# A hybrid attention layer on one core: load buffers in one ring, two weight loads moved back, scalings of queries and keys one step later

## The chip, the cores and the metric

The kernel runs on one core of a Trainium2 chip. The core has a matrix engine (PE in the profile; its weight loads are the row PEld), a vector engine (DVE), an activation engine (ACT), a general engine (POOL) and a queue engine (SP), which here issues nearly all DMA transfers from HBM into the on-chip SBUF. Each engine works through its own instruction list in order. They wait for one another through semaphores. The metric is the device time of one execution in microseconds, and lower is better.

## What is computed

A decoder layer for 256 tokens of width 2048, in float32: an adaLN modulation, one input projection to 9296 columns, two groups of eight heads each with a gate, and one output projection.

```python
mod = jax.nn.silu(c) @ w_ada + b_ada
shift, scale, gate = jnp.split(mod, 3, axis=-1)
h = _rms_norm(x, g_norm) * (1.0 + scale[:, None, :]) + shift[:, None, :]
proj = h @ w_in
qa, ka, va, za, q_idx, k_idx, w_idx, qb, kb, vb, zb = jnp.split(proj, COL_SPLITS, axis=-1)
...
ya = _dsa_attention(qa, ka, va, q_idx, k_idx, w_idx, _alibi_slopes(N_HEADS_A))
yb = _moba_attention(qb, kb, vb, _alibi_slopes(N_HEADS_B))
ya = ya.reshape(B, L, D_A) * jax.nn.silu(za)
yb = yb.reshape(B, L, D_B) * jax.nn.silu(zb)
y = jnp.concatenate([ya, yb], axis=-1) @ w_out
return x + gate[:, None, :] * y
```

With 256 tokens the second group sees one causal block. The first group keeps, for each query, the 64 keys that an indexer of 16 small heads scores highest. Scores get a penalty of slope times distance, and the slope of head n is 2 to the power of -(n+1).

## The kernel before

**Products.** Each float32 weight is split into two parts: a cast on ACT gives `wh` (L322) and a subtraction on DVE gives `wl` (L332). The activations are split alike (`hhi`, `hlo`). Three matmuls make one product: L774 (`wh` by `hhi`), L775 (`wl` by `hhi`) and L776 (`wh` by `hlo`). So no matmul of a weight piece beyond its L774 can run before both ACT and DVE have worked on that piece. Weights arrive in `raw` buffers of 1 MB, issued by SP (`issue`, L243). `wh` and `wl` have four buffers each.

**Modulation.** `w_ada` comes through the same `raw` buffers; DVE takes the dot product of each 128 x 2048 block with one instruction (`gemv`, L289). `between` (L182) decides after how many weight blocks (`n_kt`) these loads stand in the list of loads.

**Start.** The first row block of the input (k = 0) is used by itself, for the four groups of b1 (`zb1`, `qb1`, `kb1`, `vb1`: one quad of 128 x 512 weights in one load, pieces 0 to 3) and those of a0 (`za0`, `qa0`, `ka0`, `va0`: pieces 4 to 7). Then come pieces of two row blocks: 8 to 11 for a1, 12 for `i2` and so on. A finished sum leaves PSUM by an ACT copy (`evac`, L675) into `p_za0_0`, `p_za0_1` and so on, one for each half of the tokens. Sums have four PSUM buffers.

**Background tasks.** Beside the matmuls of a piece, one step of each background task is put out (`Bg.step`, L588). `prep` (L500) is one such task: eight squares on ACT (L506), a mean and a power on POOL (L149, L150), then eight scalings on ACT (L513); its first `yield` says how many pieces lie between. `idx_pair` (L461) copies two indexer heads out of PSUM (`qi`, L468) and makes their logits (`lg`, L474, L475). `head` (L524) runs from a transposition (`tr`) over scores (`s`, L540), a softmax on DVE and ACT (L545, L548) and a transposition (`pt`, L554) to the product with the values (`pv`, L563). For its penalty POOL makes a table `nb` (L536).

**Order.** The code's order is a wish: a scheduler with its own model of durations places each engine's instructions, and what it decided is fixed when the kernel is built. `in_order` pins some of it. The `raw` buffers are a pool of four (`rawp`) and a pool of two (`rawe`), which is given back when the first late tile is made; before that `rawe` serves the modulation loads in `EARLY`.

## Time and profile before

| | |
|---|---|
| median of three runs | 575.06 us (574.56 to 578.45) |
| profiled execution | 578.7 us, of which the traced span is 576.9 us |
| mean granted PE clock | 0.995 |
| PE busy | 553.6 us, 96% of the span |
| DVE, ACT, POOL busy | 444.5, 319.6 and 48.0 us |
| DMA | 150.09 MB, mean 260 GB/s |

The busy time of PE counts overlapping matmuls once. The profile also has a chain of waits followed back from the last instruction, a table of what each engine waited for, and the instructions in order of time. In rows of the timeline the first number is the start in us from the beginning of the span, the second the time to the end of the last of the xcount instructions in the row; what stands in brackets is the engine's idle time before the row, and who ended it.

### The profile page before, as it was taken

How to read it: one execution, taken by the hardware profiler on the slowest of the kernel's cores; microseconds unless marked ns; L12 is line 12 of the kernel's file. 1: busy time of each engine (PE TensorE's matmuls, PEld its weight loads, DVE VectorE, ACT ScalarE, POOL GpSimd, SP SyncE). 2: the span in 40 equal slices, each digit the busy share in tenths (PEclk: the TensorE clock that was granted, in tenths of full speed). 3: DMA queues.
4: the chain of work that ended last, by engine and by line, in shares of the span. 5: the costliest groups of instructions: out<-in, count | busy, mean ns of one | idle time of the engine just before them, and what ended most of it. 6: DMA issues, size and time to landing. Idle time of an engine off the chain costs nothing.

```text
span 576.9 us, 7456 instructions
## 1 busy us (share of the span) xinstructions
PE 553.6 (96%) x2658; PEld 462.7 (80%) x2658; DVE 444.5 (77%) x683; ACT 319.6 (55%) x652; POOL 48.0 (8%) x62
## 2 busy tenths in 40 slices
PE   3889999999999999999799999999999999999996
PEld 2769888888889988976577888888888888887885
DVE  4877789898898898998689996678787576458452
ACT  4588563544444353576555566646776785554340
POOL 4100000000000000102201002111110210000000
PEclk9999999999999999999989999999999999999999
DMA  8999998898898987877845376767675468445611
GB/s 293 412 350 370 361 346 326 330 360 285 314 359 318 366 326 270 268 298 279 303 152 177 129 275 235 273 221 265 226 255 201 148 231 279 146 150 190 244 37 38
DMA packets 59670, 150.09 MB, mean 260 GB/s; under 512 B 3056, under 2 KB 9456, under 8 KB 53616
## 3 DMA queue, kind: packets, MB, share of 16 engines
q1 hardware_dynamic: 58480, 147.51, 71.1%
q10 hardware_dynamic: 1152, 2.10, 1.2%
q8 instruction: 21, 0.34, 0.2%
q14 instruction: 17, 0.14, 0.1%
HBM read 147.50 MB, written 2.10 MB: 259 GB/s over the span
## 4 chain that ended last, share of the span: by engine, by line
PE 87%; ACT 4%; DVE 2%; POOL 2%; issue 2%; DMA 1%; SPq 0%; DVEq 0%; ACTq 0%
PE mm_y_o L774 5%; PE mm_y_o L776 5%; PE mm_y_o L775 5%; PE mm_h_zb L776 3%; PE mm_h_zb L774 3%; PE mm_h_zb L775 3%; PE mm_h_za L775 3%; PE mm_h_i L776 3%; PE mm_h_i L775 3%; PE mm_h_i L774 3%; PE mm_h_qb L774 3%; PE mm_h_za L776 3%; PE mm_h_qb L776 3%; PE mm_h_qb L775 3%; PE mm_h_qa L774 3%; PE mm_h_ka L775 2%
## 5 line engine op out<-in xcount | busy, mean ns | idle before, releaser
L322 ACT ACTIVATE wh<-raw 128x1024 fp32r<-128x1024 f32 (+3 forms) x192 | 188.2, 990 | 140.5 <-PE mm_y_o L776 32.9
L332 DVE TENSOR_TENSOR wl<-raw,wh 128x1024 fp32r<-128x1024 f32 (+3 forms) x192 | 215.0, 1140 | 60.5 <-ACT wh L322 59.9
L289 DVE CUSTOM_DVE_ANT_0 raw<-raw,s_row 128x2048 f32<-128x2048 f32 (+1 forms) x49 | 110.2, 2250 | 14.1 <-DMA raw<-in_w_ada_t 14.1
L774 PE MATMUL mm_y_o<-wh,yT 128*128 128x512 f32 x128 | 51.7, 404 | 0.0
L775 PE MATMUL mm_y_o<-wl,yT 128*128 128x512 f32 x128 | 49.9, 390 | 0.0
L776 PE MATMUL mm_y_o<-wh,yT 128*128 128x512 f32 x128 | 49.8, 390 | 0.0
L774 PE MATMUL mm_h_i<-wh,hhi 128*128 128x384 f32 (+1 forms) x96 | 31.7, 330 | 0.0
L775 PE MATMUL mm_h_i<-wl,hhi 128*128 128x384 f32 (+1 forms) x96 | 31.5, 328 | 0.0
L536 POOL TENSOR_SCALAR nbb<-dist 128x384 f32<-128x384 f32 x8 | 8.0, 1001 | 283.3 <-DVE mmod L289 211.2
L776 PE MATMUL mm_h_i<-wh,hlo 128*128 128x384 f32 (+1 forms) x96 | 31.4, 329 | 0.0
L776 PEld LDWEIGHTS mm_y_o<-wh,yT 128*128 128x128 f32 x128 | 24.0, 188 | 5.4 <-DVE yT L575 0.2
L774 PEld LDWEIGHTS mm_y_o<-wh,yT 128*128 128x128 f32 x128 | 24.1, 188 | 4.7 <-ACT yT L574 0.2
L775 PEld LDWEIGHTS mm_y_o<-wl,yT 128*128 128x128 f32 x128 | 24.1, 188 | 4.6
L774 PE MATMUL mm_h_qa<-wh,hhi 128*128 128x512 f32 x64 | 25.6, 409 | 0.9 <-ACT wh L322 0.9
L774 PE MATMUL mm_h_zb<-wh,hhi 128*128 128x512 f32 x64 | 26.4, 412 | 0.0
L774 PE MATMUL mm_h_vb<-wh,hhi 128*128 128x512 f32 x64 | 26.4, 412 | 0.0
L775 PE MATMUL mm_h_za<-wl,hhi 128*128 128x512 f32 x64 | 25.1, 392 | 0.9 <-DVE wl L332 0.9
L774 PE MATMUL mm_h_kb<-wh,hhi 128*128 128x512 f32 x64 | 25.7, 405 | 0.0
L775 PE MATMUL mm_h_zb<-wl,hhi 128*128 128x512 f32 x64 | 25.7, 401 | 0.0
L775 PE MATMUL mm_h_vb<-wl,hhi 128*128 128x512 f32 x64 | 25.6, 400 | 0.0
L774 PE MATMUL mm_h_qb<-wh,hhi 128*128 128x512 f32 x64 | 25.5, 401 | 0.0
L774 PE MATMUL mm_h_za<-wh,hhi 128*128 128x512 f32 x64 | 25.5, 406 | 0.0
(216 smaller groups left out, 1227.3 us busy)
## 6 DMA issues: line engine op xcount, KB each, us to landing
raw<-in_w_in SPq DMA_DIRECT2D x51, 1024.0 KB, 5.9
raw<-in_w_ada_t SPq DMA_DIRECT2D x47, 1024.0 KB, 6.2
raw<-in_w_out SPq DMA_DIRECT2D x16, 1024.0 KB, 5.0
raw<-in_w_in SPq DMA_DIRECT2D x17, 512.0 KB, 3.6
raw<-in_w_in SPq DMA_DIRECT2D x11, 768.0 KB, 4.6
x<-in_x SPq DMA_DIRECT2D x8, 256.0 KB, 6.9
xr<-in_x ACTq DMA_DIRECT2D x8, 256.0 KB, 6.5
raw<-in_w_in SPq DMA_DIRECT2D x3, 672.0 KB, 7.4
```

What stands on the lines that cost most here:

```text
L289: nc.vector.tensor_tensor_reduce(out=ld["v"], in0=ld["v"], in1=s_row[:, h0:h1], scale=1.0, scalar=0.0, op0=ALU.mult, op1=ALU.add, accum_ou ...
L322: nc.scalar.activation(hi[:, :n, :w], v, AF.Copy)
L332: nc.vector.tensor_tensor(lo[:, :n, :w], v, sb["hi"][:, :n, :w].bitcast(F32), op=ALU.subtract)
L536: nc.gpsimd.tensor_scalar(nb, dista if q[0] == "a" else dist, 2.0 ** -(hid + 1), 0.0, op0=ALU.mult, op1=ALU.add)
L774: nc.tensor.matmul(ps, a_hi, sb["hi"][:, i, :w], start=st, stop=False)
L775: nc.tensor.matmul(ps, a_hi, sb["lo"][:, i, :w], start=False, stop=False)
L776: nc.tensor.matmul(ps, a_lo, sb["hi"][:, i, :w], start=False, stop=en)
```

## The change

Six things are changed. (1) The first four modulation loads after the start are no longer all ahead of the a0 quad: two stand ahead of it, two behind. (2) The six `raw` buffers are used in turn; after the pool of two is given back, five are used in turn, four old ones and one in the late pool. (3) `prep` waits one piece longer before its scalings. (4) The `nb` tables are gone: the softmax instruction scales the distance itself, and the key's factor comes from a table of eight columns, made on POOL, of which one belongs to each head. (5) Four temporaries take other buffers: `junkx` the `u` tiles, and `qi`, `th` and the output's `o` the two `qk` buffers. (6) Since every one of these moves something in the scheduler's model, instructions change place that the diff does not touch. All L-numbers of matmuls and copies grow by ten.

```diff
-ADA_AT, ADA_FIRST, ADA_GAP, ADA_LAG, GATE_AT, GATE_GAP = 4, 4, 5.5, 2, 150, 8
-EARLY = {1, 2} | set(range(5, 2 * KT + KT * KT))
+ADA_FIRST, ADA_AT, ADA_GAP, ADA_LAG, GATE_AT, GATE_GAP = (4, 4, 8, 8), 9.5, 5.5, 2, 150, 8
...
     gneg = {}
+    steep = consts.tile([P, 8], F32, name="steep")
+    for h in range(8):
+        nc.gpsimd.memset(steep[:, h:h + 1], -(HD ** -0.5) * 2.0 ** (h + 1))
     for i, g in enumerate("ab"):
-        gt = consts.tile([P, 1], F32, name=f"gneg{g}")
-        nc.vector.scalar_tensor_tensor(gt, cc[:, 64 + 2 * i:65 + 2 * i], -(HD ** -0.5),
-                                       cc[:, 65 + 2 * i:66 + 2 * i], op0=ALU.mult, op1=ALU.mult)
+        gt = consts.tile([P, 8], F32, name=f"gneg{g}")
+        nc.gpsimd.tensor_scalar(gt, steep, cc[:, 64 + 2 * i:65 + 2 * i], cc[:, 65 + 2 * i:66 + 2 * i],
+                                op0=ALU.mult, op1=ALU.mult)
...
-            pool = rawe if ld["kind"] == "ada" and ld["to"][0] == "mod" and n_issued - n_start in EARLY else rawp
-            raw = pool.tile([P, 2048], F32, tag="raw", name=f"raw{n_issued}")
+            pool = rawe if not late_pool and n_issued % 6 > 3 else rawp
+            if late_pool and n_issued % 5 == 4:
+                raw = late_pool[0].tile([P, 2048], F32, tag="raw", bufs=1, name=f"raw{n_issued}")
+            else:
+                raw = pool.tile([P, 2048], F32, tag="raw", name=f"raw{n_issued}")
...
-            junk = work.tile([P, 512], F32, name=f"junkx{t}{j}", tag="big", bufs=2)
+            junk = u_tile(f"junkx{t}{j}")
...
-        qi = late_tiles().tile([P, L], F32, name=f"qi{p}", tag="qi")
+        qi = late_tiles().tile([P, 512], F32, name=f"qi{p}", tag="qk", bufs=2)[:, :L]
...
         rsqrt(ssq[:, 8:16], ssq[:, 0:8], HD)
-        yield 1
+        yield 2
...
-        nc.scalar.activation(qk[:, L:], pt[:, L:], AF.Copy, scale=gneg[q[0]])
-        nb = late_tiles().tile([P, 384], F32, name="nb" + name, tag="nb", bufs=2)
-        nc.gpsimd.tensor_scalar(nb, dista if q[0] == "a" else dist, 2.0 ** -(hid + 1), 0.0,
-                                op0=ALU.mult, op1=ALU.add)
+
+        nc.scalar.activation(qk[:, L:], pt[:, L:], AF.Copy, scale=gneg[q[0]][:, hid:hid + 1])
+        far = dista if q[0] == "a" else dist
...
-            nc.vector.tensor_tensor_reduce(out=ns[:, lo:hi], in0=ps[:, lo:hi], in1=nb[:, lo:hi], scale=1.0,
+            nc.vector.tensor_tensor_reduce(out=ns[:, lo:hi], in0=ps[:, lo:hi], in1=far[:, lo:hi],
+                                           scale=2.0 ** -(hid + 1),
```

Where the instructions stand on three engines, at three places, follows.

**The start.** On ACT, from the copies of `qa0` on, before:

```order
L675 ACTIVATE p_qa0_1_404<-mm_h0_qa0_1_395 128x512
L322 ACTIVATE wh8_413<-raw9_300 128x1024
L675 ACTIVATE p_ka0_0_425<-mm_h0_ka0_0_417 128x512
L675 ACTIVATE p_ka0_1_427<-mm_h0_ka0_1_418 128x512
L675 ACTIVATE p_va0_0_446<-mm_h0_va0_0_438 128x512
L322 ACTIVATE wh9_434<-raw11_304 128x1024
L675 ACTIVATE p_va0_1_448<-mm_h0_va0_1_439 128x512
L322 ACTIVATE wh10_452<-raw12_306 128x1024
L675 ACTIVATE p_za1_0_470<-mm_h0_za1_0_456 128x512
L322 ACTIVATE wh11_476<-raw13_308 128x1024
L675 ACTIVATE p_za1_1_472<-mm_h0_za1_1_457 128x512
```

The same stretch of ACT now:

```order
L685 ACTIVATE p_qa0_1_406<-mm_h0_qa0_1_397 128x512
L685 ACTIVATE p_ka0_0_434<-mm_h0_ka0_0_426 128x512
L685 ACTIVATE p_ka0_1_436<-mm_h0_ka0_1_427 128x512
L685 ACTIVATE p_va0_0_455<-mm_h0_va0_0_447 128x512
L685 ACTIVATE p_va0_1_457<-mm_h0_va0_1_448 128x512
L332 ACTIVATE wh8_422<-raw9_309 128x1024
L685 ACTIVATE p_za1_0_479<-mm_h0_za1_0_465 128x512
L685 ACTIVATE p_za1_1_481<-mm_h0_za1_1_466 128x512
L332 ACTIVATE wh9_443<-raw11_313 128x1024
L332 ACTIVATE wh10_461<-raw12_413 128x1024
L332 ACTIVATE wh11_485<-raw13_415 128x1024
```

The casts 8, 9 and 10 moved behind copies of sums: `wh8` behind both copies of `va0`, `wh9` behind both of `za1`.

On DVE, from the second modulation block's sums to the subtraction of piece 4, before:

```order
L403 TENSOR_TENSOR mmod1_310<-mmod1_310,cc_79 128x1
L289 ISA raw6_219,mmod2_313<-raw6_219,s_row_113 128x2048
L289 ISA mmod2_313 128x1
L418 TENSOR_TENSOR hlo1_337<-xnT1_248,hhi1_334 128x256
L289 ISA raw7_221,mmod2_313<-raw7_221,s_row_113 128x2048
L289 ISA mmod2_313 128x1
L332 TENSOR_TENSOR wl4_318<-raw8_223,wh4_316 128x512
```

The same stretch of DVE now:

```order
L413 TENSOR_TENSOR mmod1_315<-mmod1_315,cc_79 128x1
L342 TENSOR_TENSOR wl4_320<-raw6_228,wh4_318 128x512
L428 TENSOR_TENSOR hlo1_339<-xnT1_257,hhi1_336 128x256
L342 TENSOR_TENSOR wl5_352<-raw6_228,wh5_350 128x512
L342 TENSOR_TENSOR wl6_373<-raw6_228,wh6_371 128x512
L299 ISA raw7_230,mmod2_419<-raw7_230,s_row_113 128x2048
L299 ISA mmod2_419 128x1
L342 TENSOR_TENSOR wl7_394<-raw6_228,wh7_392 128x512
```

The two dot products stood ahead of `wl4`; now one stands behind `wl6` and the other behind `wl7`.

**The keys of b0.** On ACT, from the last square of `kb0` to the next casts, before:

```order
L506 ACTIVATE jkb013_2532,sskb0_2517<-p_kb0_1_775 128x128
L513 ACTIVATE p_kb0_0_773<-p_kb0_0_773,sskb0_2517 128x128 x3
L468 ACTIVATE qi3_2559<-ptq3_2556 128x256
L513 ACTIVATE p_kb0_0_773<-p_kb0_0_773,sskb0_2517 128x128
L513 ACTIVATE p_kb0_1_775<-p_kb0_1_775,sskb0_2517 128x128 x4
L322 ACTIVATE wh106_2605<-raw98_2398 128x1024
```

The same stretch of ACT now:

```order
L516 ACTIVATE jkb013_2541,sskb0_2526<-p_kb0_1_784 128x128
L523 ACTIVATE p_kb0_0_782<-p_kb0_0_782,sskb0_2526 128x128 x2
L332 ACTIVATE wh106_2606<-raw98_2399 128x1024
L478 ACTIVATE qi3_2568<-ptq3_2565 128x256
L523 ACTIVATE p_kb0_0_782<-p_kb0_0_782,sskb0_2526 128x128 x2
L523 ACTIVATE p_kb0_1_784<-p_kb0_1_784,sskb0_2526 128x128 x4
```

The first scaling still follows the last square, and the cast `wh106` came ahead of `qi3`.

**The last head.** On PE, from the last two matmuls ahead of the scores of `a13` to the product with its values, now (before, the twelve matmuls of `wh172` and `wl172` stood between `sa13` and `pva12`, and seven of piece 174 between `pta13` and `pva13`):

```order
L786 MATMUL mm_y8_o0_1_4381<-wh172_4650,yT5_4674 128x512
L549 MATMUL sa13_4728<-qka13_4682 128x128
L550 MATMUL sa13_4728<-qka13_4682 128x256
L573 MATMUL pva12_4741<-pTa12_4705,p_va1_0_566 128x256
L575 MATMUL pva12_4741<-pTa12_4705,p_va1_1_568 128x128
L578 MATMUL pva12_4741<-ident_81,p_za1_0_479 128x128
L578 MATMUL pva12_4741<-ident_81,p_za1_1_481 128x128
L784 MATMUL mm_y8_o1_0_4538<-wh174_4712,yT4_4585 128x512
L564 MATMUL pta13_4752<-ident_81,nsa13_4731 128x128
L785 MATMUL mm_y8_o1_0_4538<-wl174_4714,yT4_4585 128x512
L564 MATMUL pta13_4752<-ident_81,nsa13_4731 128x128 x2
```

The twelve matmuls of piece 172 now run ahead of the scores, and between scores and transposition lie `pva12` and one matmul.

## Rows read from the trace of the kernel before

**Rows 1.** The profile's chain of waits: share of the span by engine
```profile
PE 87%; ACT 4%; DVE 2%; POOL 2%; issue 2%; DMA 1%; SPq 0%; DVEq 0%; ACTq 0%
```
**Rows 2.** What PE waited for: us in total, times, longest us
```profile
PE lg L474 <- ACT qi L468: 4.4, 2, 3.2
PE mm_h_za L775 <- DVE wl L332: 0.9, 1, 0.9
PE mm_h_qa L774 <- ACT wh L322: 0.9, 1, 0.9
...
PE sb L540 <- ACT rl L477: 0.3, 1, 0.3
PE ptk L457 <- ACT kk L452: 0.2, 1, 0.2
```
**Rows 3.** Busy time by stretches: PE, PEld, DVE, ACT, POOL, granted clock, DMA share, GB/s
```profile
40.00:240.00 200.00, 199.83 (x946) 172.02 (x947) 172.84 (x201) 100.58 (x139) 1.29 (x3) 1.00 0.90 329
...
280.00:300.00 20.00, 16.61 (x78) 12.37 (x77) 12.49 (x21) 10.32 (x26) 4.18 (x2) 0.91 0.55 180
...
320.00:560.00 240.00, 239.94 (x1155) 199.95 (x1155) 170.14 (x297) 145.41 (x344) 26.93 (x24) 1.00 0.61 211
```
**Rows 4.** Timeline of ACT at the start
```profile
28.14 1.28 ACT L675 ACTIVATE p_vb<-mm_h_vb 128x512 f32<-128x512 f32 x2 [0.99 <-PE mm_h_vb L776]
...
30.82 2.19 ACT L322 ACTIVATE wh<-raw 128x512 fp32r<-128x512 f32 x4
...
38.45 0.61 ACT L675 ACTIVATE p_va<-mm_h_va 128x512 f32<-128x512 f32 x1
38.93 1.08 ACT L322 ACTIVATE wh<-raw 128x1024 fp32r<-128x1024 f32 x1
```
**Rows 5.** Timeline of DVE at the start
```profile
30.73 2.28 DVE L289 CUSTOM_DVE_ANT_0 raw<-raw,s_row 128x2048 f32<-128x2048 f32 x1
...
32.94 2.49 DVE L332 TENSOR_TENSOR wl<-raw,wh 128x512 fp32r<-128x512 f32 x4
...
38.11 1.22 DVE L332 TENSOR_TENSOR wl<-raw,wh 128x1024 fp32r<-128x1024 f32 x1
```
**Rows 6.** Timeline of PE at the start
```profile
30.95 1.16 PE L373 MATMUL ptx<-diag,x 128*128 128x128 f32 x8 [0.38 <-ACT xnT L379]
...
38.35 0.39 PE L776 MATMUL mm_h_va<-wh,hlo 128*128 128x512 f32 x1
38.58 0.63 PE L774 MATMUL mm_h_za<-wh,hhi 128*128 128x512 f32 x2
...
43.16 0.39 PE L775 MATMUL mm_h_qa<-wl,hhi 128*128 128x512 f32 x1
```
**Rows 7.** Timeline of ACT, POOL and DVE at the scalings of `kb0`
```profile
285.24 0.98 ACT L513 ACTIVATE p_kb<-p_kb,sskb 128x128 f32<-128x128 f32 x3 [4.39 <-POOL sskb L150]
...
281.26 3.94 POOL L150 TENSOR_TENSOR sskb<-sskb,mhalf 128x8 f32<-128x8 f32 x1
...
281.43 2.28 DVE L289 CUSTOM_DVE_ANT_0 raw<-raw,s_row 128x2048 f32<-128x2048 f32 x1
```
**Rows 8.** L150 on POOL by tiles: least/median/most ns, first and last start
```profile
L150 POOL TENSOR_TENSOR ssqa<-ssqa,mhalf x2: 1635/1635/1635, 409.8 to 456.4; 128x8 f32<-128x8 f32 x2
```
**Rows 9.** Busy time by stretches after the long wait, columns as in rows 3
```profile
288.00:290.00 2.00, 2.00 (x6) 1.55 (x5) 1.07 (x1) 2.00 (x3) 0.00 (x0) 0.51 0.03 11
290.00:292.00 2.00, 2.00 (x9) 1.54 (x7) 2.00 (x5) 0.59 (x2) 0.00 (x0) 0.63 0.00 0
```
**Rows 10.** Timeline of PE and ACT at the last head
```profile
515.25 0.58 PE L774 MATMUL mm_y_o<-wh,yT 128*128 128x512 f32 x1
...
519.06 0.49 PE L554 MATMUL pta<-ident,nsa 128*128 128x128 f32 x3
...
516.49 0.49 ACT L548 ACTIVATE nsa<-nsa,sta 128x256 f32<-128x256 f32 x1
...
519.66 0.48 ACT L556 ACTIVATE pTa<-pta 128x384 f32<-128x384 f32 x1
```

## The prediction on record

> **What bounds the kernel now.** I read the chain of waits first. It is PE for 87% of the span [rows 1], so time is won or lost only where PE stands still or runs slowly. The second view is PE's busy time by stretches: from 40 to 240 us PE is busy 199.83 of 200 us, from 320 to 560 us 239.94 of 240 [rows 3]. These 440 us hold nothing to win, whatever ACT, DVE, POOL or the DMA queues do there. From 280 to 300 us PE is busy only 16.61 us and its granted clock averages 0.91. The third view says what PE waited for [rows 2]: 4.4 us for copies of indexer heads (`qi`) in two places, 3.2 and 1.2 us long; twice 0.9 us at the start for a subtraction and a cast; 0.3 and 0.2 us at two small places. The reader is to see how little this is: 6.7 us in all, about 1.2% of the time, and every edit has to be priced against these few waits or against new ones.

> The long wait is told by its rows [rows 7]. ACT has put the eight scalings of `kb0` right behind their squares, sits idle for 4.39 us until POOL's power ends, does three scalings, and only then copies `qi`. [...]

> **The change, part by part.** *The start.* The a0 quad stands two modulation loads earlier and DVE subtracts `wl4` before the two dot products instead of after them. Before, the first cast starts only at about 30.82 us, and `wl4` at 32.94, behind a dot product of 2.28 us [rows 4, 5]. Now one small copy lies between the copies of `vb1`, which end at 28.14 + 1.28 = 29.4, and the cast of piece 4: the cast (2.19 / 4 = 0.55) ends near 30.4, `wl4` (2.49 / 4 = 0.62) near 31.05. From there 22 matmuls at 0.23 (38.35 to 38.58 [rows 6]) and one transposition of the input, 0.9 by the stretch that starts at 30.95, take PE to the end of `va0` at about 37.0. Before, its last matmul starts at 38.35. So PE gains 1.5 us here.

> Then it loses more. `wh8` now stands behind both copies of `va0`. The second sum is done at 37.3, its copy (0.61 [rows 4], less a little overlap) at 37.9, and the cast of 1024 columns (1.08) at 38.95. PE has nothing to do from 37.0 to 38.95: 1.9 us. The two matmuls with `wh8` end at 39.4, but `wl8` (1.22 [rows 5]) only at 40.15: 0.75 us. Ten matmuls lead to 42.45. `wh9` stands behind both copies of `za1`, so: sum 42.65, copy 43.2, cast 44.25, another 1.8 us of idle PE. Two matmuls, 0.5 us of waiting for `wh10`, one matmul, and `wl9` is used first at 45.45. Before, it is used first at 43.16 [rows 6], with one matmul (0.23) less done by then. The start thus costs 45.45 - 0.23 - 43.16 = **+2.1 us**. Bounds: 0, if copies overlap so well that the lead of 1.5 lasts, and +3.8, if one of the gaps also brings 1.7 us of half clock. The gaps of 1.9 lie nearer to the 1.2 that brought no fall than to the 3.2 that did, so I take 2.1.

> [...]

> *Scalings later.* For `qb0` the extra step works: casts 99 and 100 now run while ACT would wait for POOL, and `qi1` has one cast of 1.05 less ahead of it. I take -0.95 of the 1.2 us wait (bounds 0 and -1.2). For `kb0` it does not: the scheduler still has the first scaling right behind the last square, so the 4.39 us stay. Moreover `wh106` (1.08) now stands ahead of `qi3`, in place of one scaling (0.98 / 3 = 0.33): **+0.7 us** (0 to +1.1), and the half clock stays. Heads also run one piece later; transpositions and scores thus leave the place where the 0.3 us wait was: -0.3 (0 to -0.3). Casts 94 and 95 go ahead of the key's copy `kk`, which frees the 0.2.

> *The last head.* Its scores now come behind piece 172. From the end of the scores (515.25) to the end of the second exponential (516.49 + 0.49) lie 1.7 us [rows 10]. The old cover was 3.8 us (to 519.06): 12 matmuls, 2.75, and `pva12`, 1.05. Now it is `pva12`, two matmuls and one transposition, about 1.6. The copy `pTa` ends at 520.14, some 0.85 after the transpositions; now three matmuls (0.7) stand there. Together with a semaphore or two **+0.5 us** (0 to +1.3, if a cast of 1.06 comes in between on ACT). Behind it nothing waits, so it reaches the end.

> *At nothing.* The ring: transfers are not among PE's waits [rows 2], and the later loads of the start are wanted 4 us or more after the buffer before them comes free. If one were late, PE would wait for up to a whole block: 1.05 MB at the 329 GB/s of the long stretch, 3.2 us. `nb` and the key's factors: they free POOL and cost it some memsets, while the heads' stretch has PE busy 239.94 of 240; bounds 0 and -0.1. The moved temporaries lie under the same cover.

> [...]

> Sum: +2.1 - 0.95 + 0.7 - 0.3 - 0.2 + 0.5 = +1.85 us. On the profiled execution this is 578.7 + 1.85 = 580.55; that one lies 3.6 above the median of the three runs, so for the median I say 575.06 + 1.85 = 576.9.

> **The rivals.** *The start keeps its lead.* If ACT's copies of `va0` and `za1` overlap with the matmuls and casts 8 and 9 end a microsecond earlier each, the start costs nothing: 574.8. For it: the two old waits of 0.9 are gone. Against it: the order in which the copies stand.

> *The long wait goes.* If the scalings of `kb0` no longer hold up `qi3`, the 3.2 us and the 1.7 of half clock vanish and the +0.7 with them: 576.9 - 5.6 = 571.3. Only with a free start as well would it be 569.2. A smaller form: the power beside no dot product takes 1.64 instead of 3.94; the wait is 2.3 shorter and the clock may hold: 572.9 to 574.6. Against both: the order of ACT and that of DVE, where the dot product still follows the sums of heads 4 and 5.

> *The start falls to half clock (slower).* Between 37.0 and 45.45 us PE would be idle for 5 of 8.4 us, in four pieces. If gaps of this size bring the fall that the one of 3.2 us brought, half clock comes once or twice, +1.7 each: 578.6 to 580.3, and with the upper bound of the last head 581.1. It decides from the second fall on. [...]

> *The change does nothing measurable.* The terms have both signs and each is under half a per cent; with the runs of one kernel spread from 574.56 to 578.45, 575 is as good an answer as 577.

> **How the numbers follow.** A measurement of this kernel can tell about 1%, 5.75 us, from no change. Forecast (575.5 to 579): 0.5. Start keeps its lead, or nothing: 0.2, within 1%. Long wait gone or shorter: 0.14, of which half goes beyond 1% with a free start or a lucky median: 0.07 faster, 0.07 within. Half clock at the start: 0.16, of which 0.12 beyond 580.8, since a slow run can be the median. So faster 0.08, same 0.8, slower 0.12. The range from 571.3 (long wait gone) to 581.1 (second fall and the last head) leaves out less than 2 in 10. The forecast's own is 575.5 to 579.

> **What would show it.** Right: in the profile after, PE waits near 37, 42.5 and 45 us for casts on ACT, 1.5 us or more each for two of them; the wait for `qi` at 269 us is under 0.5; the one at 287 us is 3.5 to 4.3 with ACT again waiting for POOL, and half clock behind it; the last head has waits of a few tenths near 520 us. Wrong: no idle PE between 37 and 46 us, a granted clock under 1 there, no long wait at 287 us, or PE waiting for a DMA anywhere, which the ring would then have caused.

## The result, and the profile after

| | before | after |
|---|---|---|
| median of six runs | 575.6 us (574.56 to 578.45) | 584.12 us (580.0 to 585.99) |
| profiled execution | 578.7 us | 585.07 us |
| span, granted PE clock | 576.9 us, 0.995 | 583.3 us, 0.98 |
| busy PE, DVE, ACT, POOL | 553.6, 444.5, 319.6, 48.0 us | 557.9, 443.1, 319.6, 32.2 us |

The ratio of the times is 1.0132, with an interval of 1.0102 to 1.0162 (the quotient of the two medians is 1.0148). The kernel became slower by 1.3%. The prediction said 576.9 us and at most 581.1, so it was wrong.

The medians lie 8.5 us apart, the profiled executions 6.4: that of before is one of its longer ones. The six times of after spread from 580.0 to 585.99, and one of these executions is traced. What follows explains the 6.4 us between two traced executions.

The chain of waits by engine, to be set beside [rows 1]:

```profile
PE 89%; ACT 4%; POOL 2%; DVE 1%; DMA 1%; issue 1%; SPq 0%; DVEq 0%; ACTq 0%
```

What PE waited for in the kernel after (us in total, times, longest us); this answers [rows 2]:

```profile
PE lg L484 <- ACT qi L478: 5.5, 2, 2.8
...
PE mm_h_za L784 <- ACT wh L332: 1.7, 1, 1.7
PE mm_h_qa L784 <- ACT wh L332: 1.6, 1, 1.6
PE mm_h_i L785 <- DVE wl L342: 0.7, 1, 0.7
PE mm_h_za L785 <- DVE wl L342: 0.5, 1, 0.5
PE mm_h_ka L784 <- ACT wh L332: 0.2, 1, 0.2
```

These are 10.2 us, where before had 6.7 (the waits ahead of the first products, for the modulation and the first transpositions, are left out of both). Of the 6.4 us between the two profiled executions they explain 3.5 at first sight. The clock adds to them. Busy time of the kernel after by stretches (columns as in [rows 3]: us, then PE, PEld, DVE, ACT, POOL, granted clock, DMA share, GB/s):

```profile
40.00:240.00 200.00, 197.31 (x919) 168.32 (x918) 169.42 (x197) 99.00 (x132) 0.00 (x0) 0.99 0.91 332
320.00:560.00 240.00, 240.00 (x1162) 200.30 (x1161) 173.15 (x323) 145.97 (x350) 11.88 (x12) 1.00 0.60 206
...
260.00:280.00 20.00, 17.25 (x73) 12.90 (x72) 16.77 (x25) 11.70 (x36) 6.09 (x2) 0.83 0.61 213
280.00:300.00 20.00, 17.23 (x80) 12.75 (x79) 12.01 (x18) 12.01 (x36) 4.19 (x2) 0.91 0.72 263
```

The heads' stretch holds nothing, as before. What is new are two stretches with a clock below 1. The same view in steps of 2 us shows both, first at the start, then behind the wait for `qi`:

```profile
44.00:46.00 2.00, 1.79 (x5) 1.31 (x5) 2.00 (x3) 1.26 (x2) 0.00 (x0) 0.65 0.22 36
46.00:48.00 2.00, 2.00 (x6) 1.52 (x6) 2.00 (x2) 0.60 (x1) 0.00 (x0) 0.50 0.92 310
48.00:50.00 2.00, 2.00 (x10) 1.61 (x9) 1.11 (x2) 0.60 (x1) 0.00 (x0) 1.00 0.94 352
274.00:276.00 2.00, 1.93 (x9) 1.28 (x10) 2.00 (x2) 1.21 (x3) 0.00 (x0) 0.50 0.00 0
276.00:278.00 2.00, 2.00 (x6) 1.52 (x6) 2.00 (x5) 0.62 (x2) 0.00 (x0) 0.50 0.87 250
278.00:280.00 2.00, 2.00 (x6) 1.61 (x5) 2.00 (x4) 0.00 (x0) 0.00 (x0) 0.50 1.05 409
```

At half clock (granted clock 0.50) PE is 100% "busy" and does about half the work: 6 matmuls in 2 us where 10 or 11 stand at a clock of 1.00. So the busy column hides it. The first fall costs 0.35 x 2 + 0.5 x 2 = 1.7 us, the second 3 x 0.5 x 2 = 3 us. With the 3.5 us of waits this is more than 6.4; an earlier beginning and smaller places take the excess off again.

**Where the time went.** The same matmul is looked up in both traces and its two starts are subtracted. This gives a ledger of PE's delay (start before, start after, difference, in us; pieces of one group are counted through):

```
41st transposition of the input      28.62   27.54   -1.09
first matmul of i                    50.87   53.86   +3.00
17th matmul of qb                    88.97   92.98   +4.00
33rd matmul of qb                   228.89  232.89   +4.00
logits before qb0's wait            261.10  264.47   +3.37
logits behind qb0's wait            269.07  274.07   +4.99
transposition after the half clock  272.80  280.57   +7.78
logits behind kb0's wait            286.54  293.82   +7.28
last part of the program            534.27  540.63   +6.36
```

So: start +4.0 (its beginning, 1.1 earlier, is already taken off), then -0.6 up to `qb0`, +1.6 in its wait and +2.8 in the half clock behind it, -0.5 in the wait of `kb0`, -0.9 behind that, and nothing at the last head. The sum is +6.4, which is 585.07 less 578.7. The loss has two places, the start and `qb0`. The earlier beginning need not come from the change: a second execution of before, shown below, is 0.9 us early at the same transposition, and against that one the start costs +4.9.

**The start.** PE's timeline in the kernel after, where it waits, beside [rows 6]:

```profile
37.98 0.73 PE L784 MATMUL mm_h_za<-wh,hhi 128*128 128x512 f32 x2 [1.67 <-ACT wh L332]
39.23 0.50 PE L785 MATMUL mm_h_za<-wl,hhi 128*128 128x512 f32 x1 [0.53 <-DVE wl L342]
...
43.42 0.73 PE L784 MATMUL mm_h_qa<-wh,hhi 128*128 128x512 f32 x2 [1.63 <-ACT wh L332]
44.37 0.62 PE L784 MATMUL mm_h_ka<-wh,hhi 128*128 128x512 f32 x1 [0.21 <-ACT wh L332]
...
61.15 0.45 PE L785 MATMUL mm_h_i<-wl,hhi 128*128 128x384 f32 x1 [0.74 <-DVE wl L342]
```

The four gaps at 38 to 44 us stand where they were forecast and have nearly the forecast lengths (1.9, 0.75, 1.8, 0.5). The half clock follows them directly. The wait at 61.15 was not foreseen: the subtraction that it needs stands behind a dot product of 2.29 us on DVE, which starts at 57.93 behind `hlo` of the second modulation chunk.

**The scalings.** The first group shows POOL's power (L152) at `qb0`, ACT's scalings that wait for it, DVE's instructions beside it, and PE's wait that follows. Below it stand the power and the dot product at `kb0`, which answer [rows 7]:

```profile
262.85 5.77 POOL L152 TENSOR_TENSOR ssqb<-ssqb,mhalf 128x8 f32<-128x8 f32 x1
...
268.65 1.28 ACT L523 ACTIVATE p_qb<-p_qb,ssqb 128x128 f32<-128x128 f32 x4 [4.13 <-POOL ssqb L152]
...
261.69 1.40 DVE L489 SCALAR_TENSOR_TENSOR sc<-rl,w,sc 128x128 f32<-128x128 f32 x4
263.01 0.69 DVE L531 SCALAR_TENSOR_TENSOR p_zb<-thb,p_zb 128x512 f32<-128x512 f32 x1
263.62 3.49 DVE L342 TENSOR_TENSOR wl<-raw,wh 128x1024 fp32r<-128x1024 f32 x3
...
274.07 0.81 PE L484 MATMUL lg<-kiT,qi 64*128 64x128 f32 x4 [2.75 <-ACT qi L478]
...
287.88 3.95 POOL L152 TENSOR_TENSOR sskb<-sskb,mhalf 128x8 f32<-128x8 f32 x1
...
288.05 2.28 DVE L299 CUSTOM_DVE_ANT_0 raw<-raw,s_row 128x2048 f32<-128x2048 f32 x1
```

The power on 128x8 numbers takes 1.64 us alone [rows 8]. Here it takes 5.77, and it ends at 268.62, 1.5 us after the third subtraction `wl` ends at 267.11. During all that time DVE goes from one instruction with two SBUF inputs to the next without a pause; the short `sc`, beside the last of which the power starts, has two as well (`rl` and `sc`). In the kernel before, the power at `qb0` took only 2.51 us. ACT starts the scalings late, the next `qi` comes behind them, PE is idle for 2.75 us, and the half clock follows.

### The profile page after: what moved, and what is told of

It is laid out like the page before. It is cut to its first block, busy times and chain, and to the rows that moved or that the text cites. A ratio compares the mean times of both kernels' runs of the same rounds, so it can differ in the third digit from the quotient of the medians.

```text
span 583.3 us, 7421 instructions
## 1 busy us (share of the span) xinstructions
PE 557.9 (96%) x2658; PEld 465.5 (80%) x2658; DVE 443.1 (76%) x681; ACT 319.6 (55%) x652; POOL 32.2 (6%) x56
## 4 chain that ended last, share of the span: by engine, by line
PE 89%; ACT 4%; POOL 2%; DVE 1%; DMA 1%; issue 1%; SPq 0%; DVEq 0%; ACTq 0%
PE mm_y_o L784 5%; PE mm_y_o L785 5%; PE mm_y_o L786 5%; PE mm_h_zb L784 3%; PE mm_h_za L785 3%; PE mm_h_zb L785 3%; PE mm_h_ka L785 3%; PE mm_h_zb L786 3%; PE mm_h_qa L785 3%; PE mm_h_qa L786 3%; PE mm_h_za L786 3%; PE mm_h_qb L784 3%; PE mm_h_qb L786 3%; PE mm_h_ka L786 3%; PE mm_h_ka L784 2%; PE mm_h_va L784 2%
## 5 line engine op out<-in xcount | busy, mean ns | idle before, releaser
L784 PE MATMUL mm_h_ka<-wh,hhi 128*128 128x512 f32 x64 | 25.8, 408 | 0.2 <-ACT wh L332 0.2
L785 PE MATMUL mm_h_qa<-wl,hhi 128*128 128x512 f32 x64 | 25.7, 402 | 0.0
L786 PE MATMUL mm_h_kb<-wh,hlo 128*128 128x512 f32 x64 | 25.7, 402 | 0.0
L786 PE MATMUL mm_h_qa<-wh,hlo 128*128 128x512 f32 x64 | 25.7, 402 | 0.0
L785 PE MATMUL mm_h_kb<-wl,hhi 128*128 128x512 f32 x64 | 25.7, 401 | 0.0
```

Source lines behind the costliest of these rows:

```text
L784: nc.tensor.matmul(ps, a_hi, sb["hi"][:, i, :w], start=st, stop=False)
L785: nc.tensor.matmul(ps, a_hi, sb["lo"][:, i, :w], start=False, stop=False)
L786: nc.tensor.matmul(ps, a_lo, sb["hi"][:, i, :w], start=False, stop=en)
```

## The experiments

For the start one reason stood first: the split of the modulation loads alone, through its gaps and the half clock. For `qb0` two were set against each other. One said that the later scalings let two casts through, whose subtractions then run beside the power. The other said that the scalings have no part in it, and that another of the edits moved instructions on DVE.

**Only the split, in the kernel before.** Only the places of the modulation loads are those of the kernel after:

```diff
-ADA_AT, ADA_FIRST, ADA_GAP, ADA_LAG, GATE_AT, GATE_GAP = 4, 4, 5.5, 2, 150, 8
+ADA_FIRST, ADA_AT, ADA_GAP, ADA_LAG, GATE_AT, GATE_GAP = (4, 4, 8, 8), 9.5, 5.5, 2, 150, 8
...
```

> The kernel before with the two modulation loads moved behind the a0 quad, and nothing else. Its order on ACT and DVE up to 60 us is that of the changed kernel, behind it that of the kernel before. Theory 1 (the start's loss comes from the order that the split brings): waits of about 1.7, 0.5 and 1.6 us at 36 to 44 us, half clock near 45 us, PE about 4.0 us late from 62 us on and to the end, so +3 to +4.5 us on the median. Rival (the loss comes from the ring, whose loads start later): no such waits, within 1 us of before.

Measured: 580.08 us against 575.41, ratio 1.008 (1.0052 to 1.0107). PE shows the gaps of the kernel after, 1.67, 0.52, 1.63, 0.22 and later 0.74, and the half clock behind them. By stretches, columns as above:

```profile
46.00:48.00 2.00, 2.00 (x6) 1.52 (x6) 2.00 (x3) 0.31 (x1) 0.00 (x0) 0.50 0.55 149
```

From 62 to 260 us each matmul starts 5.07 later than in before. The split alone costs 4.7 us in the medians, and that is the start of the kernel after: its profiled execution lacks the earlier beginning, hence 5.07 instead of 4.0.

**Only the later scalings, in the kernel before.**

```diff
         rsqrt(ssq[:, 8:16], ssq[:, 0:8], HD)
-        yield 1
+        yield 2
```

> The kernel before with the scalings one step later, and nothing else. Theory 2 (POOL's power stands still while DVE subtracts): casts 99 and 100 and their subtractions lie beside the power of qb0, which takes 4.5 to 6 us instead of 2.5; PE waits some 2.7 us instead of 1.1 for qi near 269 us and falls to half clock; +3.5 to +4.5 us behind it, about +0.5 more or less at the keys; in all +3 to +5 us. Rival (the longer power comes from the moved temporaries or the missing nb tables): the power stays at 2.5 us, and the time gains up to 1 us.

Measured: 576.44 us, ratio 1.0006 (0.9986 to 1.0026). The power at `qb0` stays short, and `qi` is hardly late there (0.18 instead of 1.13 us). But at `kb0` the cast of piece 106 stands between the scalings and `qi`. POOL at `qb0`, and ACT at `kb0`:

```profile
259.24 2.51 POOL L150 TENSOR_TENSOR ssqb<-ssqb,mhalf 128x8 f32<-128x8 f32 x1
...
282.20 0.69 ACT L513 ACTIVATE p_kb<-p_kb,sskb 128x128 f32<-128x128 f32 x2 [2.18 <-POOL sskb L150]
282.80 1.04 ACT L322 ACTIVATE wh<-raw 128x1024 fp32r<-128x1024 f32 x1
283.74 0.36 ACT L468 ACTIVATE qi<-ptq 128x256 f32<-128x256 f32 x1
```

So the -0.95 of the prediction is real, and it is given back at `kb0`, where PE waits 2.82 us. The later scalings by themselves don't lengthen the power, so the theory that they do failed.

**The kernel after without these two edits**, so with the ring, without the tables, and with the temporaries moved:

```diff
-ADA_FIRST, ADA_AT, ADA_GAP, ADA_LAG, GATE_AT, GATE_GAP = (4, 4, 8, 8), 9.5, 5.5, 2, 150, 8
+ADA_FIRST, ADA_AT, ADA_GAP, ADA_LAG, GATE_AT, GATE_GAP = (4, 4, 4, 4), 9.5, 5.5, 2, 150, 8
...
-        yield 2
+        yield 1
```

> The changed kernel with both other parts undone: the four early modulation loads ahead of the quad as before, the scalings one step after the squares as before. What is left is the ring, the tables gone from POOL and the moved temporaries. Both theories: within 1 us of before, with the gain of up to 1 us at kk and at the scores near 300 us. Rival (the ring or the temporaries carry part of the loss): slower by 2 us or more.

Measured: 581.59 us, ratio 1.0103 (1.0077 to 1.013). Both theories had this at about nothing, as the prediction had, and both were wrong; the rival, 2 us or more, was right. POOL, ACT and DVE at `qb0`:

```profile
257.56 6.83 POOL L152 TENSOR_TENSOR ssqb<-ssqb,mhalf 128x8 f32<-128x8 f32 x1
...
264.43 2.16 ACT L523 ACTIVATE p_qb<-p_qb,ssqb 128x128 f32<-128x128 f32 x7 [6.12 <-POOL ssqb L152]
...
256.41 1.40 DVE L489 SCALAR_TENSOR_TENSOR sc<-rl,w,sc 128x128 f32<-128x128 f32 x4
257.73 0.68 DVE L531 SCALAR_TENSOR_TENSOR p_zb<-thb,p_zb 128x512 f32<-128x512 f32 x1
258.33 2.35 DVE L342 TENSOR_TENSOR wl<-raw,wh 128x1024 fp32r<-128x1024 f32 x2
260.60 2.28 DVE L299 CUSTOM_DVE_ANT_0 raw<-raw,s_row 128x2048 f32<-128x2048 f32 x1
```

Again the power ends (264.39) 1.5 us after the last instruction of the row (260.60 + 2.28). PE waits 4.71 us for `qi`. So the loss at `qb0` comes from the edits that were priced at nothing.

**The kernel after with `qi` in its own buffers again.** DVE's order pointed to one of the temporaries. `qi` and `th` share two buffers in the kernel after, so the second `thb` can be written only when the logits have read the `qi` before it: on ACT it starts at 259.02, behind logits that start at 258.00, while with `qi` in its own buffers it starts at 254.31, ahead of the logits at 255.84. The product `p_zb` comes behind `thb`. A dot product that had stood behind `p_zb` then runs ahead of it.

```diff
-        qi = late_tiles().tile([P, 512], F32, name=f"qi{p}", tag="qk", bufs=2)[:, :L]
+        qi = late_tiles().tile([P, L], F32, name=f"qi{p}", tag="qi")
```

> The changed kernel with one temporary moved back: qi has buffers of its own again and no longer shares two with th. The order on DVE before the power of qb0 becomes that of the kernel before (a dot product and two subtractions behind it, no run of short score updates). Theory 3 (sharing the buffers is what brought the short updates beside the power): the power of qb0 takes 2.5 us instead of 5.8, the wait for qi near 270 us shrinks from 2.75 to under 0.5 us, no half clock there, -4 to -5 us against the changed kernel, so about 579 to 580. [...]

Measured: 577.58 us, ratio to before 1.0031 (1.0014 to 1.0048), so 6.5 us less than the kernel after; 4 to 5 had been expected. POOL and DVE at `qb0` in this kernel:

```profile
261.42 2.51 POOL L152 TENSOR_TENSOR ssqb<-ssqb,mhalf 128x8 f32<-128x8 f32 x1
...
257.07 0.68 DVE L531 SCALAR_TENSOR_TENSOR p_zb<-thb,p_zb 128x512 f32<-128x512 f32 x1
...
258.99 2.29 DVE L299 CUSTOM_DVE_ANT_0 raw<-raw,s_row 128x2048 f32<-128x2048 f32 x1
261.20 3.50 DVE L342 TENSOR_TENSOR wl<-raw,wh 128x1024 fp32r<-128x1024 f32 x3
```

And in the kernel before:

```profile
260.17 2.51 POOL L150 TENSOR_TENSOR ssqb<-ssqb,mhalf 128x8 f32<-128x8 f32 x1
...
257.13 0.68 DVE L521 SCALAR_TENSOR_TENSOR p_zb<-thb,p_zb 128x512 f32<-128x512 f32 x1
257.74 2.29 DVE L289 CUSTOM_DVE_ANT_0 raw<-raw,s_row 128x2048 f32<-128x2048 f32 x1
259.95 2.36 DVE L332 TENSOR_TENSOR wl<-raw,wh 128x1024 fp32r<-128x1024 f32 x2
```

In both a dot product is the last instruction ahead of the subtractions, and the power starts 0.22 us after the first subtraction has started. It ends 1.5 us after that first one, although further ones follow. In the two slow cases the power starts beside the last short `sc`, 0.16 and 0.17 us ahead of `p_zb`, and ends only after the whole row of instructions.

The same edit in the kernel without the split and with `yield 1`:

> The run that left only the rest of the change (581.6 us), with qi moved back to its own buffers: ring, no nb tables, th and o in the qk buffers, junkx in u tiles. Theory 3 (the shared buffers are the whole loss of the rest): 574 to 575.5, the power of qb0 2.5 us. Rival (ring or tables cost as well): above 576.5.

Measured: 575.18 us instead of 581.59; ratio to before 0.9998 (0.997 to 1.0026), the power 2.51 us. So the shared buffers of `qi` were the whole loss of the rest; the ring, the tables and the other temporaries together move the median by nothing that can be measured.

**The dot product at `kb0` with one SBUF input, in the kernel before.** This was to test that it is the second input that holds up the power. The sum leaves out the product with the conditioning vector for this block:

```diff
+        if ld is loads[100]:
+            nc.vector.tensor_reduce(mod[kind, c][:, i:i + 1], ld["v"], axis=mybir.AxisListType.X, op=ALU.add)
+        else:
...
```

> The kernel before, but one dot product of the gate (the one beside the power of kb0 at 281 us) is a sum over the weight block alone: it reads one tensor in SBUF instead of two. This leaves out the product with the conditioning vector for one of 16 blocks of the gate. Theory 2 (two inputs in SBUF keep POOL out): the sum takes about as long, yet the power beside it ends after about 1.6 us instead of 3.9; the wait for qi falls from 3.2 to about 1 us, half clock goes away or shrinks; -2.3 to -4 us. Rival (any DVE work beside it slows the power, or it is long by itself): 3.9 us as before, no change.

Measured: 574.84 us, ratio 0.9985 (0.9965 to 1.0004). In its trace the power runs beside a sum of the same length and isn't held up:

```profile
281.04 1.75 POOL L150 TENSOR_TENSOR sskb<-sskb,mhalf 128x8 f32<-128x8 f32 x1
...
281.47 2.29 DVE L290 TENSOR_REDUCE mgate<-raw 128x1 f32<-128x2048 f32 x1 [0.18 <-DMA raw<-in_w_ada_t]
```

PE then waits 1.09 us for `qi` instead of 3.24, there is no half clock, and later matmuls start 4.0 us earlier than in the profiled execution of before. But the median moves by only 0.6. Why, the next run shows. It also takes away the proof: the sum starts 0.43 us after the power, and a two-input product that starts as late, 0.44 us after it in the kernel after with `qi` back, doesn't hold up the power either (1.75 us).

**The kernel before once more**, unchanged:

> The kernel before, unchanged, to see a second execution of it. Theory 2 (the power of kb0 loses to the dot product in some executions only): about 573 to 575 us, the power takes 1.7 instead of 3.9 us, the wait for qi near 287 us is 1.1 instead of 3.2 and no half clock follows; or, one time in five, the same picture as before. Rival (the wait of 3.2 us belongs to every execution): 3.9 us of power again at any total time.

Measured: 577.1 us, and in its trace the power and the dot product at `kb0` stand so:

```profile
279.29 1.40 DVE L479 SCALAR_TENSOR_TENSOR sc<-rl,w,sc 128x128 f32<-128x128 f32 x4
...
280.43 1.75 POOL L150 TENSOR_TENSOR sskb<-sskb,mhalf 128x8 f32<-128x8 f32 x1
...
280.68 2.29 DVE L289 CUSTOM_DVE_ANT_0 raw<-raw,s_row 128x2048 f32<-128x2048 f32 x1
```

The same program, the same two instructions: 1.75 us here, 3.94 in the execution on which the prediction was built. There the dot product started 0.17 us after the power [rows 7], here 0.25. The twelve traces that have this dot product (or the sum) there all sort that way: 0.17 us in four (before, after, the kernel without the two edits, and the last kernel below) with 3.94 or 3.95 us, and 0.24 to 0.62 us in eight (one of them the sum with one input) with 1.74 or 1.75.

What makes the 0.17 or the 0.24 stands in the same traces. The power starts 0.22 to 0.24 us into the last short `sc` each time, and that `sc` ends 0.25 us after the power's start. In the four long cases DVE goes on without a pause; the weight block of the dot product had landed 0.5 us before it in the execution of the prediction, and 1.6 us before it in the kernel after. In the eight short ones DVE pauses, by 0.06 us or more, and the power ends 1.5 us after the `sc`; in the four with the longest pauses, 0.18 to 0.38 us, what ends the pause is the landing of the block. In the execution of the prediction, and in the kernel after with `qi` back:

```profile
280.11 1.40 DVE L479 SCALAR_TENSOR_TENSOR sc<-rl,w,sc 128x128 f32<-128x128 f32 x4
...
282.52 2.29 DVE L299 CUSTOM_DVE_ANT_0 raw<-raw,s_row 128x2048 f32<-128x2048 f32 x1 [0.19 <-DMA raw<-in_w_ada_t]
```

So the long wait at `kb0` is a collision that happens in some executions of a kernel and not in others, and what goes with it is a load that lands in time; in the traces where DVE had to wait for a late one the power took 1.75 us at most. Among the 23 times of before beside the kernel with one input, 6 were 577.5 us or more, and of the ten times with one input none was over 575.28. That this upper group is the collision fits, but isn't shown: this very run of before took 577.1 without it, having lost about 3 us further on, 2 of them in three waits of PE near 412, 428 and 434 us.

**The start with a fixed order.** The kernel with `qi` back, and casts, subtractions and copies of sums held in the order of the code for pieces 4 to 12 (`PIN0` and `PIN1`), so that the cast of piece 8 doesn't stand behind the copies of `va0`:

```diff
-        cast_hi(j + LA)
-        cast_lo(j + LA)
+        with (in_order() if PIN0 <= j <= PIN1 else nullcontext()):
+            cast_hi(j + LA)
+            cast_lo(j + LA)
...
-            evac(ld)
+            with (in_order() if PIN0 <= j <= PIN1 else nullcontext()):
+                evac(ld)
```

> As the run with qi moved back, and in addition the casts and the copies of sums of pieces 4 to 12 keep the order in which the code writes them: wh8 ahead of the copies of ka0, wh9 ahead of those of va0, wh10 ahead of those of za1. The two modulation loads stay behind the quad. Theory 1 (the casts behind the copies are the loss at the start): the waits of 1.7 and 1.6 us near 36 and 42 us go, half clock at 45 us goes, one wait of 0.7 to 1.5 us for wl8 behind two dot products remains; -4 to -5.5 us against the run with qi moved back, 574 to 576. Rival (the early quad itself is the loss, DVE having idled while it could do dot products): 2 us or less gained.

Measured: 574.41 us, ratio 0.9976 (0.9954 to 0.9998), 3.2 us less than without the fixed order; 4 to 5.5 had been expected. Of the waits for weights at the start one of 2.3 us and one of 0.3 are left, both for subtractions, and the clock stays at 1.00 there:

```profile
PE mm_h_za L787 <- DVE wl L343: 2.3, 1, 2.3
```

So it isn't the split by itself that costs most, but the place of ACT's copies that came with it.

**Versions beyond both kernels.** The split undone, `qi` back, and the later scalings for the queries alone, since they gain at `qb0` and lose at `kb0`:

```diff
-        yield 2
+        yield 2 if c == "q" else 1
```

> The changed kernel with the modulation loads ahead of the quad as before, qi in its own buffers, and the later scalings for queries alone. What is left: ring, no nb tables, th and o in the qk buffers, junkx in u tiles, later scalings of queries. Theories 1 and 3: none of the losses is left; the earlier start of the transpositions (-1.3) and the wait at 269 us shorter by 0.9 are; 572.5 to 574.5. Rival (something else in the rest costs): 575 or more.

Measured: 573.76 us, ratio 0.9965 (0.9944 to 0.9986), as expected.

The same, and the dot product at `kb0` held back behind the subtraction of piece 106:

```diff
-        flush_gemv()
+        if j >= 109 or loads[100] not in gemv_todo:
+            with (in_order() if loads[100] in gemv_todo else nullcontext()):
+                flush_gemv()
...
-        cast_lo(j + LA)
+        with (in_order() if j + LA == 106 else nullcontext()):
+            cast_lo(j + LA)
```

> As the run before, and the dot product that lies beside the power of kb0 is pinned behind the next subtraction. Theory 2 (DVE instructions with two inputs in SBUF keep POOL's power waiting, in some executions and not in others): the upper group of times, some 3.5 us above the lower, disappears, the lowest stays within 1 us of the run before, and the largest is within 2 us of the lowest; median 571.5 to 574. Rival (the upper group comes from the clock or DMA): the spread stays.

Measured: 576.93 us, ratio 1.0016 (0.9995 to 1.0037). A miss. The power at `kb0` takes 1.75 us, but the spread (574.77 to 578.65) isn't smaller: 3 of the 12 times are 577.5 us or more with no dot product beside the power. That speaks for the rival, another source of the upper group. But the trace also has a new wait of 2.3 us for ACT's copy of a head, besides one of the same size at the start, for a load that landed late, so this run doesn't decide it.

The version with 573.76 us again, now with the fixed order at the start:

> The kernel with the losses undone (modulation loads ahead of the quad, qi back, later scalings for queries only), and casts and copies of pieces 4 to 12 pinned in the order of the code. Theory 1: at the old order of loads the casts stood well already; the two waits of 0.9 and 0.4 us become at best 0.5: 573 to 574, no difference to the run without the pin. Rival (pinning is worth several us by itself): 571 or less.

Measured: 573.02 us (572.18 to 575.44), ratio 0.9952 (0.9932 to 0.9972). This is faster than both kernels. The longest wait of its PE, apart from those for the modulation and the transpositions of the input at the very start, is one of 1.6 us for a `qi`.

And with the split kept, the order fixed and the later scalings for the queries alone:

> The whole change but three things: qi in its own buffers, the casts of pieces 4 to 12 pinned, and the later scalings for queries only. The modulation loads stay split around the quad. Theories 1 and 3: about 0.6 us better than the pinned run with later keys (574.4), as the cast ahead of qi3 goes: 573 to 574.5, faster than before. Rival (the split costs even when pinned): 575 or more.

Measured: 574.07 us, ratio 0.998 (0.9957 to 1.0003), so with the order fixed the split costs about 1 us in the medians, which the intervals don't separate. Its profiled execution is its slowest, 577.83, and it has the collision at `kb0`: the power 3.94 us, PE's wait 3.7, and a clock of 0.50 from 284 to 290 us.

## Why the prediction was wrong, by its own steps

**What bounds the kernel: right.** PE still sets the time, the heads' stretch holds nothing, and what changed lies in a few waits and the clock behind them.

**The start, +2.1, measured +4.0.** The four gaps were right in place and nearly in size. The term failed in two points. The half clock, 1.7 us by the clock of 0.51 and 0.63 behind the long wait [rows 9] ((0.49 + 0.37) x 2), was put aside because the gaps were "nearer to the 1.2 that brought no fall" (around that wait, from 262 to 276 us, the clock of before is 1.00); it came in the profiled executions of after and of the split alone, 0.50 from 46 to 48 us in both. The upper bound, +3.8, had named it. And the wait of 0.74 at 61 us was not looked for: the sum ended at the first use of `wl9`, although DVE had a dot product of 2.28 us still to place. That the transpositions began 1.1 us earlier made up for part of it; against the second execution of before the start costs 4.9.

**`qb0`, -0.95, measured +4.4.** This is the step that failed most. The gain itself was right; the later scalings alone take the wait from 1.13 to 0.18 us. But the power's price was taken to stay at that of before. The prediction compared the power with its neighbour on DVE only at `kb0` (3.94 us beside a dot product, 1.64 alone [rows 7, 8]), and did not ask at `qb0` what the change puts beside it. There `sc` and `p_zb` fall behind the dot product, right beside the power, which takes 5.77 us instead of 2.51. The bounds, 0 and -1.2, held no loss.

**"At nothing": wrong for `qi`.** "The moved temporaries lie under the same cover" looked at what they cost in the heads' stretch. Their cost was elsewhere: two tiles that share buffers add a wait, the wait moves a product on DVE, and this costs 6.5 and 6.4 us in two kernels. For the ring, the tables and the other temporaries together the step was right, and PE waits for no DMA.

**`kb0`, +0.7, measured -0.5.** The order was right: ACT waits 4.39 us for POOL, and the cast stands ahead of `qi`. PE's wait is 2.77 instead of 3.24 all the same. The larger error lies behind the term: the 3.24 us were taken as a property of the kernel, and they belong to a collision that other executions don't have. The prediction held against its rival that in DVE's order the dot product still follows the sums. This isn't enough: with the dot product behind the sums the power took 3.94 or 3.95 us in four traces and 1.75 at most in eight, and with the long ones went a load that had landed in time. That the profiled execution lay 3.6 us above the median was the sign, and it was only subtracted.

**The last head, +0.5, measured 0**; PE doesn't wait there. The two small terms, -0.3 and -0.2, came to -1.5 with what else lies at their places.

**The rivals.** "The start falls to half clock" was right in what it named, with a chance of 0.16. Its times, 578.6 to 581.1, hold that of the split alone (580.08). That 0.12 of the 0.16 lay beyond 580.8 doesn't follow from these times, of which only the top does. What lies above them is the power at `qb0`, for which there was no rival.

**The collision.** Every power of `qb0` and `kb0` that took over 2 us, 2.51 to 6.83, started inside a DVE instruction with two SBUF inputs. That the second input matters isn't shown, since the sum with one input started too late, 0.43 us after the power, to matter. Nor do the listed starts tell which of the two goes first: in the long cases at `kb0` the power is 0.17 us ahead of the next DVE instruction and still ends 1.5 us behind it, and at `qb0` of the kernel after it ends 1.5 us behind the whole row.

## What to carry to other kernels

An edit that only lets two tiles share a buffer still adds a wait, and where a scheduler places the instructions it can move others beside a short instruction that a third engine waits for; so compare the neighbours of each such instruction, also where the diff doesn't touch it. When the profiled execution lies well above the median, find out which of its waits the other executions don't have, before a term is built on one. Then undo the edits one at a time: here the sharing of one buffer cost 6.5 us and the split of the loads 4.7, and the best version, at 573.02 us, does without both and fixes the order at the start. Such prices hold beside what else is in the kernel and needn't add up: with `qi` back, the split and the later scalings together cost 2.4 us (577.58 against 575.18).

## What the runs showed of the hardware

**The same gaps brought half clock in one execution and not in another.** At the start, with gaps of 1.67, 0.53, 1.63 and 0.21 us, the clock fell to 0.50 in the kernel after, and with the split alone. With `qi` back the gaps are the same to 0.01 us, and the clock stays at 1.00:

```profile
44.00:46.00 2.00, 1.93 (x8) 1.53 (x9) 2.00 (x3) 1.11 (x3) 0.00 (x0) 1.00 0.23 41
46.00:48.00 2.00, 2.00 (x11) 1.64 (x10) 2.00 (x2) 1.05 (x2) 0.00 (x0) 1.00 0.99 365
```

At `kb0` a wait of 2.82 us (only the later scalings) left the clock at 1.00 from 280 to 300 us, while one of 2.20 (`qi` back) took its mean there to 0.91. So the length of the last gap alone doesn't decide it, and what does stays open. For a sum this means that both outcomes belong into the range of a gap of the sizes seen here, 1.6 to 2.8 us.
